# A hybrid attention and RWKV-7 layer on one core: two sets of turned tiles made by VectorE squares and quadrant copies instead of TensorE transposes

## The chip, the cores and the metric

The kernel runs on one core of one Trainium2 chip. The metric is the device time of one execution in microseconds (us). Beside the times there is one profiled execution of the kernel before. Engines are named as in the profile: PE is TensorE (PEld its weight loads), DVE is VectorE, ACT is ScalarE, POOL is GpSimd, SP is the queue that issues nearly all DMAs. L566 is line 566 of the kernel before.

## What is computed

One layer over 256 frames of width 4096, in float32. A single input projection feeds 16 heads of softmax attention with a forget gate, 32 heads of RWKV-7 time mixing (as 16 pairs of 64 wide heads), and a SiLU gate. The gated outputs go through an output projection, then a residual LayerNorm.

```
proj = einsum('bsd,dc->bsc', x, w_in)
logits[t,s] = q_t.k_s/sqrt(128) + sum_{s<j<=t} log f_j      (s <= t)
fox = softmax(logits) @ v
S_t = S_{t-1} diag(decay_t) + (S_{t-1} a_t) b_t^T + v_t k_t^T ;  y_t = S_t r_t
h   = concat(fox, groupnorm(y)*gain + bias + bonus) * silu(z)
x   = LayerNorm(ALPHA*x + h @ w_out)
```

## The kernel before

The input projection is one long stream of matrix products. It is cut into 8 pairs of heads (`n` = 0 to 7) of 4 blocks each (`b` = 0 to 3), and a block into 16 weight tiles (`q`). Block 0 of a pair gives r and k of the RWKV heads, block 1 gives v of both kinds, blocks 2 and 3 give q, k and the gates of the attention heads 2n and 2n+1. Each weight tile is 128x1024 float32. It is loaded by a DMA on SP (`load`, L215), split into a rounded high part by ScalarE (L139, `w_..h`) and a remainder by VectorE (L140, `w_..l`), and used by 12 products of 128x128 on 128x512 (L145 to L147): two of them take the high part for each product that takes the remainder. Four high parts and three remainders can exist at a time, so that the splits run up to three tiles ahead of TensorE. Behind the 8 pairs the output projection follows as a stream of the same kind (`wo`, L872 to L874).

All other work is written as generators, the "sides". `slot()` (L195) lets each of them take one step, and is called after every sixth product of the stream. `yield from wait(n)` therefore lets n slots, or 6n products, pass before the next operation of that side is issued. The table `W` (L46) holds such waits. Each engine then runs its own instructions in one fixed order; a scheduler at build time sets that order, keeping to the program's order for the most part but drawing some instructions forward.

Two sides matter here.

- `rwkv(n)` (L517) handles the RWKV heads of a pair. The chunk factors are in `BK` (128 partitions, 2 halves `u`, 4 chunks `c`, 128 columns). Products `gp` (L531) use them as they are; then POOL scales the first three chunks in place (L533, `kept`). After `W["tp"]` = 4 slots TensorE transposes all eight 128x128 pieces into PSUM (`tp`, L566) and ScalarE copies them out as `BKt` (L567). Then follow the wait `W["d1"]`, 31 steps of a triangular inversion on VectorE (`prod`, `xc`, L595 and L598), one per slot, further products, and for each of the chunks 0 to 2 a product `sp` (L680) that reads `BKt`.
- `fox(i, ...)` (L727) is one attention head. Products `fsp` (L736, L737) give the logits in three 128x128 blocks; VectorE and ScalarE turn them into probabilities in `lg` (L742 to L746). After `W["fp"]` = 5 slots from there TensorE transposes the three blocks into PSUM (`fpt`, L750), ScalarE copies them out as `pT` (L752), and after `W["fo"]` = 3 slots the products `fop` (L756, L757) apply the probabilities to v.

`ident` is an identity matrix, `flat(t)` joins the last two dimensions of a tile, P is 128, B is 32 and NCH is 4. `pst` takes one of five PSUM buffers. `spread` and `gather_heads` already use VectorE's transpose of 32x32 squares, and `gather_heads` (L457) already copies 32 partitions to another 32 on POOL.

Of the kernel before, what the change touches and what calls it, by code (L numbers as in the profile page):

```python
# [10 lines left out]
F32 = mybir.dt.float32  # L11
# [6 lines left out]
P = 128  # L18
# [5 lines left out]
NCH = S // C  # L24
# [18 lines left out]
LAND = 3  # L43
SENT = 3
BEHIND = 13
W = {"fo": 3, "vs": 2, "np": 4, "gp": 5, "tp": 4, "d1": 8, "d2": 12, "xp": 3, "fs": 4, "fp": 5}  # L46
NB = D // OB

PAR = ["w0", "a0", "k_k", "k_a", "r_k", "gn_gain", "gn_bias", "mu_r", "mu_k", "mu_v"]
# [1 line left out]
B = 32  # L51
# [33 lines left out]
def layer(ctx: ExitStack, tc: tile.TileContext, xt, xtok, w_main, w_lora, w_first, muv, w_o, up, par, mulora, fbias, lng, lnb, cst, out):  # L85
    nc = tc.nc
# [8 lines left out]
    def pst(name):  # L95
        return ps.tile([P, 512], F32, tag="ps", name=name)
# [34 lines left out]
    ident = cs[:, C_ID : C_ID + P]  # L131
# [56 lines left out]
    def wait(n):  # L188
        for _ in range(n):
            yield  # L190
# [67 lines left out]
    rp = mid.enter_context(tc.tile_pool(name="rp", bufs=1))  # L258
# [6 lines left out]
    def t256(tag, name, bufs=1):  # L265
        return rp.tile([P, S], F32, tag=tag, name=name, bufs=bufs)
# [103 lines left out]
    def gate(y, key, k):  # L370
        far = k < FAR
        while len(storing) > 1:
            yield
        h = rp.tile([P, S], F32, tag="h", name=f"h{k}")
        nc.vector.scalar_tensor_tensor(h, y, 0.5, szs[key], ALU.mult, ALU.mult)
        pool, tag, bufs = (rp, "hl", 2) if far else (xpool, f"x{k}", 1)
        hl = pool.tile([P, 2, S], F32R, tag=tag, name=f"hl{k}", bufs=bufs)
        nc.scalar.copy(hl[:, 0, :], h)
        nc.vector.tensor_tensor(hl[:, 1, :], h, hl[:, 0, :].bitcast(F32), ALU.subtract)
        if far:  # L380
            storing.append(k)
            yield from wait(SENT)
            issue(hd[k], flat(hl).bitcast(F32))
            kept_h.add(k)
            storing.remove(k)
        else:
            ht[k] = hl
# [3 lines left out]
    def ch(t):  # L391
        return t.rearrange("p (c t) -> p c t", t=C)

    def flat(t):
        return t.rearrange("p a b -> p (a b)")
# [67 lines left out]
    def left(t, j):  # L463
        return t.rearrange("p u c (x j t) -> p u c j x t", x=2, j=2)[:, :, :, j]

    def prepare(i):
# [30 lines left out]
        for j in range(2):  # L497
            h = HALF[j]
            nc.vector.tensor_tensor(BK[h, :, KB[j][1]], ch(k)[h], ch(eI)[h], ALU.mult)
        yield from wait(W["np"] if n else 2 * W["np"])  # L500
        nc.vector.tensor_tensor(hr[:, 0, :], hr[:, 0, :], hr[:, 1, :], ALU.add)
# [15 lines left out]
    def rwkv(n):  # L517
# [4 lines left out]
        lc, BK, LT, bon = q["lc"], q["BK"], q["lt"], q["bon"]  # L522
        lt = [left(LT, j) for j in range(2)]
        yield from wait(W["gp"])
        gp = [[pst(f"gp{n}_{u}_{j}") for j in range(2)] for u in range(2)]
# [18 lines left out]
        nb = rp.tile([P, 2, B, B], F32, tag="Nb", name=f"Nb{n}")  # L544
# [14 lines left out]
        SV = [SVt[:, :, :, j, :] for j in range(2)]  # L559
        UV = [UVt[:, :, :, j, :] for j in range(2)]  # L560
        yield from wait(W["tp"])
        BKt = rp.tile([P, 2, NCH, P], F32, tag="shl", name=f"BKt{n}")
        for u in range(2):
            tp = pst(f"tp{n}_{u}")
            for c in range(NCH):
                nc.tensor.transpose(tp[:, c * P : (c + 1) * P], BK[:, u, c, :], ident)  # L566
            nc.scalar.copy(flat(BKt[:, u]), tp)  # L567
        yield from wait(W["d1"])

        def turns():  # L570
# [41 lines left out]
        for j in range(2):  # L612
# [8 lines left out]
            nc.gpsimd.memset(SV[j][HALF[j], :, 0, :], 0.0)  # L621
        yield from wait(W["d2"] - 1)
        for a in range(4):
# [4 lines left out]
        for u in range(2):  # L628
            for c in range(NCH):
                for j in range(2):  # L630
                    a, b = slice(C * j, C * j + B), slice(C * j + B, C * j + C)
                    nc.tensor.matmul(qp[b, u * P + c * B : u * P + (c + 1) * B], gb[j][a, u, c, B:C], T[a, u, c, :], start=True, stop=True)
        Q = rp.tile([P, 2, NCH, B], F32, tag="xc", name=f"Q{n}")
        for j in range(2):
            b = slice(C * j + B, C * j + C)
# [13 lines left out]

        yield from wait(W["xp"])  # L650
        xp = pst(f"xp{n}")
        for u in range(2):
            for c in range(NCH):
                for j in range(2):
                    a, b = slice(C * j, C * j + B), slice(C * j + B, C * j + C)
                    nc.tensor.matmul(xp[a, u * P + c * B : u * P + (c + 1) * B], Q[b, u, c, :], X[b, u, c, C * j + B : C * j + C], start=True, stop=True)
        for j in range(2):
            a = slice(C * j, C * j + B)
# [68 lines left out]
    def fox(i, q, k, vt):  # L727
        nb = rp.tile([P, 3, P], F32, tag="nb", name=f"nb{i}")
        row = ncd[i : i + 1, :]
        nc.sync.dma_start(out=flat(nb[:, 0:1, :]), in_=row[:, :P].to_broadcast([P, P]))  # L730
        nc.sync.dma_start(out=flat(nb[:, 1:3, :]), in_=row.to_broadcast([P, S]))
        for m in (0, 2):
            nc.gpsimd.affine_select(out=nb[:, m, :], in_=nb[:, m, :], compare_op=ALU.is_ge, fill=NEG, base=0, pattern=[[-1, P]], channel_multiplier=1)  # L733
        yield from wait(W["fs"])
        sp = pst(f"fsp{i}")
        nc.tensor.matmul(sp[:, :P], q[:, :P], k[:, :P], start=True, stop=True)  # L736
        nc.tensor.matmul(sp[:, P : 3 * P], q[:, P:], k, start=True, stop=True)  # L737
        lg = rp.tile([P, 3, P], F32, tag="lg", name=f"lg{i}")
        spv = sp[:, : 3 * P].rearrange("p (a t) -> p a t", t=P)
        st = rp.tile([P, 6], F32, tag="fst", name=f"fst{i}", bufs=2)  # L740
        for m, blk in enumerate((slice(0, 1), slice(1, 3))):
            nc.vector.scalar_tensor_tensor(lg[:, blk, :], spv[:, blk, :], ct[:, m * NF + i : m * NF + i + 1], nb[:, blk, :], ALU.add, ALU.add)  # L742
            nc.vector.tensor_reduce(st[:, m : m + 1], lg[:, blk, :], AX.XY, ALU.max, negate=True)
            nc.scalar.activation(lg[:, blk, :], lg[:, blk, :], AF.Exp, bias=st[:, m : m + 1], accum_out=st[:, 2 + m : 3 + m])
            nc.vector.reciprocal(st[:, 4 + m : 5 + m], st[:, 2 + m : 3 + m])
            nc.vector.tensor_scalar(lg[:, blk, :], lg[:, blk, :], st[:, 4 + m : 5 + m], None, ALU.mult)  # L746
        yield from wait(W["fp"])
        pt = pst(f"fpt{i}")
        for m in range(3):
            nc.tensor.transpose(pt[:, m * P : (m + 1) * P], lg[:, m, :], ident)  # L750
        pT = rp.tile([P, 3 * P], F32, tag="nb", name=f"pT{i}")
        nc.scalar.copy(pT, pt[:, : 3 * P])  # L752
        yield from wait(W["fo"])
        op = pst(f"fop{i}")
        f = slice(i % 2 * P, i % 2 * P + P)
        nc.tensor.matmul(op[:, :S], vt[:, 0, f], pT[:, :S], start=True, stop=False)  # L756
        nc.tensor.matmul(op[:, P:S], vt[:, 1, f], pT[:, S:], start=False, stop=True)  # L757
        o = t256("fq", f"fo{i}")
        nc.scalar.copy(o, op[:, :S])
        while f"f{i}" not in szs or 2 * i >= FAR and not closed:  # L760
            yield
        yield from gate(o, f"f{i}", 2 * i)
        foxed.add(i)
# [6 lines left out]
    def chain():  # L770
        while not ff:
            yield
        yield from forget()
        for n in range(G // 2):
            yield from rwkv(n)
# [12 lines left out]
    def unload(n, b, bk, vt):  # L788
# [43 lines left out]
        else:  # L832
# [4 lines left out]
            yield from wait(LAND - 1)  # L837
        nc.scalar.mul(fq, fq, FOX_SCALE)
        side(fox(i, fq, fk, vt))
        yield  # L840
        silu2(zf, f"f{i}")
# [91 lines left out]
    for b, q in outs:  # L933
        if q == 0:
            pool, tag = (ps, "ps") if b == 1 or b and b % 2 == 0 else (pp, "pp")
# [47 lines left out]
    def moments(m):  # L983
        mv = rpool.tile([P, 2], F32, name=f"mv{m}")
        sd = rpool.tile([P, 1], F32, name=f"sd{m}")
        rs = rpool.tile([P, 1], F32, name=f"rs{m}")
        s2 = rpool.tile([P, 1], F32, name=f"s2{m}")
        zh = rpool.tile([P, 1], F32R, name=f"zh{m}")
        z = factors(m, "d")
        nc.gpsimd.memset(z[:, 3:5], 1.0)  # L990
        za = factors(m, "a") if m else None
        add(m, NB - 1)
        nc.vector.bn_aggr(mv, st[m].rearrange("p b s -> p (b s)"))
        mean = mv[:, 0:1]
        nc.scalar.activation(sd, mv[:, 1:2], AF.Sqrt, bias=lneps)
        nc.vector.reciprocal(rs, sd)
        nc.vector.tensor_tensor(s2, mean, rs, ALU.mult)
        nc.vector.tensor_copy(zh, s2)
        nc.vector.tensor_copy(z[:, 0:3:2], zh.bitcast(F32).to_broadcast([P, 2]))
        last = nc.vector.tensor_tensor(z[:, 1:2], s2, zh.bitcast(F32), ALU.subtract)  # L1000
        if m:
            for n, (v, at) in enumerate(((mean, (slice(0, 3, 2), slice(1, 2))), (sd, (slice(3, 5), slice(5, 6))))):
                h = rpool.tile([P, 1], F32R, name=f"zah{n}")
                nc.scalar.copy(h, v)
                nc.scalar.copy(za[:, at[0]], h.bitcast(F32).to_broadcast([P, 2]))
                nc.scalar.activation(za[:, at[1]], h.bitcast(F32), AF.Identity, scale=-1.0, bias=v)
        rss.append(rs)
        return z, za, last.ins
# [18 lines left out]
    z0, _, last = moments(0)  # L1027
# [23 lines left out]
    for n in range(HALVED):  # L1051
        b = HALVED + n
# [57 lines left out]
```

## Time and profile before

| | us |
|---|---|
| three timed runs | 1934.82, 1935.48, 1938.32; median 1935.48 |
| the profiled execution's own time | 1936.05 |
| its span in the trace | 1934.3 |
| granted TensorE clock, mean | 0.999 of full speed |

The profiled execution took 1.75 us more than its span, which is work outside the recorded stretch. The busy shares of the page say which engine has the most to do, and the list of waits says whether that engine ever stood still; the timeline gives starts in us from the beginning of the span, then durations in us. In the timeline neighbouring equal instructions are merged into one line with their count. A matrix product is listed with a duration that is longer than the distance to the next one, since products overlap.

### The profile page before, as it was taken

The numbers are of one execution on the slowest core, as the hardware profiler recorded it, in microseconds if no ns is written. First come the engines' busy times: TensorE is split into PE (matmuls) and PEld (weight loads), VectorE is DVE, ScalarE is ACT, GpSimd is POOL, SyncE is SP. The second block draws the span as 40 slices with busy tenths as digits, with TensorE's granted clock in tenths as the row PEclk, the third lists the DMA queues.
The fourth block names the chain that finished last, engine by engine and source line by source line (L and its number), as shares of the span: only waits on it lengthen the run. The fifth ranks groups of instructions, "written<-read, shape, count | busy, mean of one in ns | idle before, by whom it ended". The sixth has DMA issues, their size and how long they took to land.

```text
span 1934.3 us, 27820 instructions
## 1 busy us (share of the span) xinstructions
PE 1920.1 (99%) x9897; PEld 1592.7 (82%) x9897; DVE 1362.9 (70%) x2323; ACT 964.2 (50%) x1447; POOL 123.6 (6%) x207
## 2 busy tenths in 40 slices
PE   9999999999999999999999999999999999999998
PEld 9887788888888888888888888888888888888886
DVE  6676777867785778577957795779577856755555
ACT  6554464456444644564446444645454554443332
POOL 0020002000200020002000200020001001000000
PEclk9999999999999999999999999999999999999999
DMA  9577766867786778677867676777677777766564
GB/s 343 151 237 209 220 203 203 241 196 215 214 234 196 216 208 240 190 220 207 235 191 224 208 230 198 223 218 214 207 214 220 241 273 251 245 200 197 186 204 166
DMA packets 269391, 420.04 MB, mean 217 GB/s; under 512 B 142338, under 2 KB 169364, under 8 KB 269252
## 3 DMA queue, kind: packets, MB, share of 16 engines
q1 hardware_dynamic: 268820, 417.58, 70.6%
q8 instruction: 77, 1.26, 0.3%
q10 hardware_dynamic: 432, 0.69, 0.1%
q14 instruction: 62, 0.51, 0.1%
HBM read 388.55 MB, written 29.64 MB: 216 GB/s over the span
## 4 chain that ended last, share of the span: by engine, by line
PE 95%; DVE 2%; DMA 2%; ACT 0%; issue 0%; SPq 0%; DVEq 0%; ACTq 0%
PE acc L145 23%; PE acc L147 23%; PE acc L146 23%; PE oacc L872 6%; PE oacc L874 6%; PE oacc L873 6%; PE up L671 1%; PE gp L531 1%; PE rh L641 1%; PE sp L680 1%; DMA Nb<-nd 0%; PE accl L147 0%; PE accl L146 0%; PE accl L145 0%; PE yp L702 0%; PE yp L700 0%
## 5 line engine op out<-in xcount | busy, mean ns | idle before, releaser
L598 DVE TENSOR_REDUCE xc<-prod 128x8 f32<-128x16 f32 (+30 forms) x248 | 73.1, 295 | 6.5
L595 DVE TENSOR_TENSOR prod<-Nb,xc 128x8 f32<-128x8 f32 (+30 forms) x248 | 71.4, 288 | 6.5 <-DMA Nb<-nd 0.2
L140 DVE TENSOR_TENSOR w_6l<-w,w_6h 128x1024 fp32r<-128x1024 f32 x31 | 37.9, 1221 | 43.1 <-ACT w_6h L139 29.2
L140 DVE TENSOR_TENSOR w_5l<-w,w_5h 128x1024 fp32r<-128x1024 f32 x31 | 41.3, 1333 | 28.2 <-PE acc L147 25.8
L733 POOL TENSOR_SCALAR_AFFINE_SELECT nb<-nb 128x128 f32<-128x128 f32 x32 | 13.8, 436 | 710.3 <-DMA nb<-ncd 265.7
L140 DVE TENSOR_TENSOR w_12l<-w,w_12h 128x1024 fp32r<-128x1024 f32 x31 | 37.9, 1223 | 27.7 <-issue 14.4
L140 DVE TENSOR_TENSOR w_10l<-w,w_10h 128x1024 fp32r<-128x1024 f32 x31 | 37.9, 1222 | 24.3 <-issue 19.7
L139 ACT CAST w_5h<-w 128x1024 fp32r<-128x1024 f32 x31 | 32.6, 1052 | 42.8 <-PE acc L146 37.6
L140 DVE TENSOR_TENSOR w_8l<-w,w_8h 128x1024 fp32r<-128x1024 f32 x31 | 37.8, 1219 | 20.2 <-PE acc L147 10.5
L139 ACT CAST w_13h<-w 128x1024 fp32r<-128x1024 f32 x31 | 32.5, 1047 | 38.0 <-PE acc L146 16.9
L140 DVE TENSOR_TENSOR w_0l<-w,w_0h 128x1024 fp32r<-128x1024 f32 x31 | 37.9, 1223 | 19.1 <-PE acc L147 17.8
L140 DVE TENSOR_TENSOR w_7l<-w,w_7h 128x1024 fp32r<-128x1024 f32 x31 | 37.9, 1221 | 19.0 <-PE acc L147 13.1
L139 ACT CAST w_12h<-w 128x1024 fp32r<-128x1024 f32 x31 | 32.5, 1048 | 37.4 <-DMA w<-in_w_main_dram 21.9
L140 DVE TENSOR_TENSOR w_4l<-w,w_4h 128x1024 fp32r<-128x1024 f32 x31 | 37.8, 1219 | 18.8 <-issue 11.8
L140 DVE TENSOR_TENSOR w_11l<-w,w_11h 128x1024 fp32r<-128x1024 f32 x31 | 37.8, 1220 | 18.1 <-PE acc L147 18.1
L140 DVE TENSOR_TENSOR w_1l<-w,w_1h 128x1024 fp32r<-128x1024 f32 x31 | 37.9, 1223 | 17.9 <-PE acc L147 17.6
L145 PE MATMUL acc<-w_8h,x 128*128 128x512 f32 x124 | 50.4, 407 | 0.0
L145 PE MATMUL acc<-w_7h,x 128*128 128x512 f32 x124 | 49.8, 402 | 0.2 <-ACT w_7h L139 0.2
L145 PE MATMUL acc<-w_5h,x 128*128 128x512 f32 x124 | 49.8, 402 | 0.0
L145 PE MATMUL acc<-w_15h,x 128*128 128x512 f32 x124 | 49.6, 400 | 0.0
L147 PE MATMUL acc<-w_1l,x 128*128 128x512 f32 x124 | 48.5, 391 | 1.1 <-DVE w_1l L140 1.1
L145 PE MATMUL acc<-w_3h,x 128*128 128x512 f32 x124 | 49.5, 399 | 0.0
(814 smaller groups left out, 6543.3 us busy)
## 6 DMA issues: line engine op xcount, KB each, us to landing
w<-in_w_main_dram SPq DMA_DIRECT2D x496, 512.0 KB
wo<-in_w_o_dram SPq DMA_DIRECT2D x128, 512.0 KB
bt<-bk SPq DMA_DIRECT2D x88, 128.0 KB
Nb<-nd SPq DMA_DIRECT2D x16, 512.0 KB
hd<-hl SPq DMA_DIRECT2D x29, 256.0 KB
h<-hd SPq DMA_DIRECT2D x29, 256.0 KB
wr<-in_w_first_dram SPq DMA_DIRECT2D x15, 384.0 KB
lr<-in_w_lora_dram SPq DMA_DIRECT2D x14, 336.0 KB
```

What stands on the lines that cost most here:

```text
L139: nc.scalar.copy(hi[:, :n], src[:, :n])
L140: nc.vector.tensor_tensor(lo[:, :n], src[:, :n], hi[:, :n].bitcast(F32), ALU.subtract)
L145: nc.tensor.matmul(acc[:, :n], xs[k][:, 0, tt], hi[:, o : o + n], start=(k == 0), stop=False)
L146: nc.tensor.matmul(acc[:, :n], xs[k][:, 1, tt], hi[:, o : o + n], start=False, stop=False)
L147: nc.tensor.matmul(acc[:, :n], xs[k][:, 0, tt], lo[:, o : o + n], start=False, stop=(k == KT - 1))
L531: nc.tensor.matmul(o, BK[h, u, c, :], lt[j][h, u, c], start=True, stop=True)
L595: first = nc.vector.tensor_tensor(prod[:, :, :, s + 1 :], nb[:, :, s : s + 1, s + 1 :].to_broadcast([P, 2, NJ, w]), xc[:, :, :, s + 1 :], ...
L598: nc.vector.tensor_reduce(xc[:, :, :, s : s + 1], prod[:, :, :, s:], AX.X, ALU.add)
L641: nc.tensor.matmul(rh[:, u * P : (u + 1) * P], LT[:, u, c, 0:P], flat(SVt[:, u, c]), start=True, stop=True)
L872: nc.tensor.matmul(acc, ht[k][:, 0, tt], hi, start=(k == 0), stop=False)
L873: nc.tensor.matmul(acc, ht[k][:, 1, tt], hi, start=False, stop=False)
L874: nc.tensor.matmul(acc, ht[k][:, 0, tt], lo, start=False, stop=(k == KT - 1))
```

## The change

The two sets of TensorE transposes go. In `rwkv`, VectorE transposes the 32x32 squares of the first three chunks of `BK` in place, once for each `u`. Then 16 POOL copies, one for each pair of a source and a target group of 32 partitions, move the squares to their places in `BKt`, which holds three chunks instead of four. The side yields after 8 of them and again after 16. In `fox`, VectorE transposes the squares of all three blocks of `lg` in place, and 16 copies, taken in turn by ScalarE and POOL, make `pT`. The wait `W["fo"]` ahead of the `fop` products grows from 3 to 7 slots. No PSUM buffer is taken for either set any more.

```diff
-W = {"fo": 3, "vs": 2, "np": 4, "gp": 5, "tp": 4, "d1": 8, "d2": 12, "xp": 3, "fs": 4, "fp": 5}
+W = {"fo": 7, "vs": 2, "np": 4, "gp": 5, "tp": 4, "d1": 8, "d2": 12, "xp": 3, "fs": 4, "fp": 5}
...
-        BKt = rp.tile([P, 2, NCH, P], F32, tag="shl", name=f"BKt{n}")
+        BKt = rp.tile([P, 2, NCH - 1, P], F32, tag="shl", name=f"BKt{n}")
         for u in range(2):
-            tp = pst(f"tp{n}_{u}")
-            for c in range(NCH):
-                nc.tensor.transpose(tp[:, c * P : (c + 1) * P], BK[:, u, c, :], ident)
-            nc.scalar.copy(flat(BKt[:, u]), tp)
+            v = flat(BK[:, u, : NCH - 1, :])
+            nc.vector.transpose(v, v)
+        for a in range(4):
+            for b in range(4):
+                nc.gpsimd.tensor_copy(BKt[B * b : B * (b + 1), :, :, B * a : B * (a + 1)], BK[B * a : B * (a + 1), :, : NCH - 1, B * b : B * (b + 1)])
+            if a % 2:
+                yield
         yield from wait(W["d1"])
...
-        pt = pst(f"fpt{i}")
-        for m in range(3):
-            nc.tensor.transpose(pt[:, m * P : (m + 1) * P], lg[:, m, :], ident)
-        pT = rp.tile([P, 3 * P], F32, tag="nb", name=f"pT{i}")
-        nc.scalar.copy(pT, pt[:, : 3 * P])
+        nc.vector.transpose(flat(lg), flat(lg))
+        pT = rp.tile([P, 3, P], F32, tag="nb", name=f"pT{i}")
+        for a in range(4):
+            for b in range(4):
+                (nc.gpsimd.tensor_copy if b % 2 else nc.scalar.copy)(pT[B * b : B * (b + 1), :, B * a : B * (a + 1)], lg[B * a : B * (a + 1), :, B * b : B * (b + 1)])
+        pT = flat(pT)
         yield from wait(W["fo"])
```

## The prediction

> **What bounds the kernel now.** I read the page first, for the busiest engine and the chain of work that ended last.
>
> ```profile
> span 1934.3 us, 27820 instructions
> PE 1920.1 (99%) x9897; PEld 1592.7 (82%) x9897; DVE 1362.9 (70%) x2323; ACT 964.2 (50%) x1447; POOL 123.6 (6%) x207
> PE 95%; DVE 2%; DMA 2%; ACT 0%; issue 0%; SPq 0%; DVEq 0%; ACTq 0%
> ```
>
> PE is the bound: 95% of the chain is PE. A busy PE can still hide stalls, so the list of PE's waits came next; its longest entries include:
>
> ```profile
> PE acc L147 <- DVE w_1l L140: 1.1, 1, 1.1
> PE acc L147 <- DVE w_8l L140: 1.0, 1, 1.0
> PE xp L656 <- DVE Q L636: 1.0, 1, 1.0
> ```
>
> Each happened once. So PE is fed nearly always, and what leaves PE's queue shortens the kernel, unless the new work elsewhere makes PE wait.
>
> **What is removed from PE.** A product's listed duration isn't its cost, so I took the distance between stream products around each group of transposes from the timeline of PE.
>
> ```profile
> 148.90 0.39 PE L146 MATMUL acc<-w_10h,x 128*128 128x512 f32 x1
> 149.13 0.39 PE L147 MATMUL acc<-w_10l,x 128*128 128x512 f32 x1
> 149.36 1.03 PE L566 MATMUL tp<-cs,BK 128*128 128x128 f32 x8
> 150.15 0.48 PE L145 MATMUL acc<-w_11h,x 128*128 128x512 f32 x1
> 150.47 0.40 PE L146 MATMUL acc<-w_11h,x 128*128 128x512 f32 x1
> ...
> 196.08 0.39 PE L147 MATMUL acc<-w_10l,x 128*128 128x512 f32 x1
> 196.31 0.49 PE L750 MATMUL fpt<-cs,lg 128*128 128x128 f32 x3
> 196.56 0.48 PE L145 MATMUL acc<-w_11h,x 128*128 128x512 f32 x1
> 196.87 0.39 PE L146 MATMUL acc<-w_11h,x 128*128 128x512 f32 x1
> ```
>
> Undisturbed stream products start 0.23 us apart. From 149.13 to 150.47 two distances (0.455) and eight transposes pass, 1.34 us: the eight cost 0.89. From 196.08 to 196.87 it is 0.79: three cost 0.34.
>
> ```profile
> L566 PE MATMUL tp<-cs,BK x64: 270/272/273, 149.4 to 1486.6; 128*128 128x128 f32 x64
> L750 PE MATMUL fpt<-cs,lg x48: 270/272/273, 196.3 to 1586.0; 128*128 128x128 f32 x48
> ```
>
> 64 transposes are 8 groups, 48 are 16 groups: 8 x 0.89 + 16 x 0.34 = 12.5 us off PE. The TensorE page of the Trainium skill ("TensorE: Matmul & The Clock Gate", Part 4: PE-mode transpose) gives about 275 ns for a transpose inside a kernel, for bf16; 112 of them would be 30.8 us, and the result 18 us below mine. The listed 272 ns agrees with it, the distances do not.
>
> **What is added elsewhere.** No DMA is added or moved; SP's queue keeps its order. The new operations' forms aren't in the trace, so their nearest rows bound them.
>
> ```profile
> L492 ACT COPY lc<-eL 128x4 f32<-128x4 f32 x16 | 3.0, 189 | 0.0
> L591 ACT COPY prod<-cs 128x128 f32<-128x128 f32 x16 | 4.0, 296 | 43.7 <-POOL vs L536 43.7
> L620 ACT COPY UV<-SV 64x512 f32<-64x512 f32 x16 | 9.9, 621 | 2.1 <-DVE SV L617 1.6
> L801 DVE STREAM_TRANSPOSE bk<-bk 128x512 f32<-128x512 f32 x44 | 30.8, 702 | 6.6 <-ACT bk L912 4.2 <-ACT bk L910 2.2
> L461 DVE STREAM_TRANSPOSE n<-hr 128x256 f32<-128x256 f32 x16 | 7.1, 442 | 0.3
> L457 POOL COPY hr<-hr x64: 192/376/1384, 99.0 to 1462.8; 32x16 f32<-32x16 f32 x64
> L437 POOL MEMSET eL<- 128x4 f32 x16 | 1.7, 109 | 296.6 <-DVE lt L493 280.8 <-DVE lt L494 15.8
> L263 POOL MEMSET gb<- 128x1024 f32 x2 | 1.9, 964 | 0.0
> ```
>
> An ACT copy of 96 elements lies between 4 and 128 elements: 0.27 us (bounds 0.19 and 0.62). A DVE turn of 384 lies midway between 256 and 512: 0.57. A POOL copy starts from 0.19 for 16 elements, and the two memsets give 0.84 ns for each further element: 0.26 for 96, 0.34 for 192. That is 16 x 0.34 = 5.4 us of POOL per pair for `BKt`, and 8 x 0.26 = 2.1 for each `pT`. The spread of L457 (192 to 1384) has a cause that the timeline shows:
>
> ```profile
> 308.73 1.21 DVE L140 TENSOR_TENSOR w_0l<-w,w_0h 128x1024 fp32r<-128x1024 f32 x1
> 308.94 3.08 POOL L457 COPY hr<-hr 32x16 f32<-32x16 f32 x4 [0.50 <-DVE hr L454]
> 310.74 1.23 DVE L140 TENSOR_TENSOR w_1l<-w,w_1h 128x1024 fp32r<-128x1024 f32 x1
> ```
>
> Four small copies take 3.08 us because two of them overlap a weight split on DVE and end only with it. This is the mechanism of the slower rival below.
>
> For `BKt` the cover is wide. DVE's turn waits for POOL's L533; behind it in DVE's queue stand the next splits, and PE waits for those.
>
> ```profile
> 519.74 1.47 POOL L533 TENSOR_TENSOR BK<-BK,lc 128x768 f32<-128x768 f32 x1 [2.97 <-PE gp L531]
> 526.11 1.21 DVE L140 TENSOR_TENSOR w_9l<-w,w_9h 128x1024 fp32r<-128x1024 f32 x1
> ```
>
> L533 ends at 521.2, and DVE comes to the two turns, which stand before `w_9l`, near 526.1: no wait. The 1.1 us by which `w_9l` moves lies inside the lead of three tiles. The copies end 5 to 22 us (16 x 1.38) later; the first `sp` comes some 54 slots (waits of 8, 12 and 3, and 31 inversion steps) of 6 x 0.2275 us later, 74 us. Cost on PE: 0. With no cover it would be up to 22 us a pair.
>
> For `pT` I followed head 4 (pair 2); the next pairs repeat it.
>
> ```profile
> 573.91 0.38 PE L736 MATMUL fsp<-fk,fq 128*128 128x128 f32 x2
> 580.72 0.34 DVE L746 TENSOR_SCALAR lg<-lg,fst 128x256 f32<-128x256 f32 x1
> 581.40 1.05 ACT L139 CAST w_14h<-w 128x1024 fp32r<-128x1024 f32 x1 [1.47 <-PE acc L146]
> 585.83 0.59 PE L756 MATMUL fop<-pT,vt 128*128 128x256 f32 x2
> ```
>
> The turn ends at 580.72 + 0.34 + 0.57 = 581.6. ACT's eight copies end at 583.8, POOL's at 583.7. `fop` now stands 12 slots behind `fsp`: 573.9 + 0.66 for `fsp` itself + 72 x 0.2275 = 590.9. Slack 7 us. Behind ACT's copies stands `w_14h`; it ends at 584.9 instead of 582.5, its remainder at 586.1, and PE reaches tile 14 one and a half tiles (18 products, 4.1 us) after 585.8, near 589.6. Hidden; the cover goes if an ACT copy takes over 0.7 us. The longer `W["fo"]` delays only the head's output, which is stored for the output projection. The two slots added to `rwkv` move its products as a whole.
>
> **Where PE does wait: the first head.** In the changed program's order of instructions the scheduler has drawn the first `fop` (n = 0) forward: it stands 16 stream products behind `fsp`, not 72. ACT's queue there has seven `pT` copies ahead of `w_9h`, which PE needs for its products 13 to 16.
>
> ```profile
> 186.50 0.74 DVE L742 SCALAR_TENSOR_TENSOR lg<-fsp,ct,nb 128x128 f32<-128x128 f32 x2 [5.88 <-PE fsp L737]
> 187.16 1.22 DVE L140 TENSOR_TENSOR w_8l<-w,w_8h 128x1024 fp32r<-128x1024 f32 x1
> 195.52 0.34 DVE L746 TENSOR_SCALAR lg<-lg,fst 128x256 f32<-128x256 f32 x1
> ...
> 186.99 0.40 PE L146 MATMUL acc<-w_8h,x 128*128 128x512 f32 x1
> 188.43 0.74 PE L147 MATMUL acc<-w_8l,x 128*128 128x512 f32 x2 [1.04 <-DVE w_8l L140]
> 191.64 0.73 PE L147 MATMUL acc<-w_9l,x 128*128 128x512 f32 x2 [0.16 <-DVE w_9l L140]
> ```
>
> In the new order DVE goes from `lg` (186.5) through two reductions (0.5 from start to start), `w_8l` (1.15) and ten short operations (1.9 in all) to the turn: 0.7 + 0.5 + 1.15 + 1.9 = 4.2, so 190.7. Check: before, 9.0 us lie between `lg` and its last scaling; without three splits, one 0.6 us product and five inversion operations that no longer stand between, 3.8 remain. The turn ends at 191.3, seven copies at 193.2, `w_9h` at 194.2. PE, out of work at 187.2, waits 1.7 us for `w_8l` (188.9), runs eight products to 190.7, waits 3.5 for `w_9h`, and finds `pT` done when it comes to `fop` at 195.1. That is 5.2 us of waiting against 1.04 + 0.16 before: +4.0 (with bounds of 0.19 and 0.62 a copy: +3.4 and +6.4; +2.9 if the turn comes 0.5 earlier).
>
> **The last pair.** There ACT's order puts five and three copies of head 15 among the readouts R and UV of the last `rwkv`, whose products follow each other a slot apart. Three copies (0.8) or a cast (1.05) can hold up one such product: +1.0 (bounds 0 and 3; the existing `xp` wait of 1.0 shows the kind).
>
> **Sum.** Against the profiled execution's own 1936.05 us: -12.5 + 4.0 + 1.0 = -7.5, so 1928.5. The median of the runs is 0.57 below that execution: 1928.0. Its own range: 12.5 - 2.9 + 1.1 (if the `w_1l` wait, too, goes with the new order) gives 1924.8; 12.5 - 6.4 - 3 gives 1932.4.
>
> **Rivals.**
>
> *POOL is locked out (slower).* If nearly each `pT` copy meets a two-input operation on DVE, as two of four `hr` copies did, eight cost up to 8 x (1.384 + 0.07) = 11.6 us instead of 2.1, and end at 593.2; `fop` stands at 590.9, so PE waits 2.3. Over the seven even heads after the first that is 16 us: 1928.0 + 16 = 1944. It decides once a copy averages over 1.16 us (9.3 us of slack for eight). For it: DVE is 70% busy, and its splits are two-input. Against it: by the `hr` rate (3.08 for four) eight take 6.2 to 6.8, 2.5 us short of the slack. The Trainium skill's "SBUF — State Buffer" (SBUF: two separate sides) says that whichever of the two starts first holds the shared ports for its whole instruction; the `hr` copies that end with the split agree.
>
> *The gain is eaten (no change).* ACT copies at 0.62, the first head's +6.4, the last pair's +3: 1932.4, and DVE held up by POOL's copies for another 1 us or so: 1933. For it: most 32-partition moves have no row of their own. Against it: ACT's time follows the elements in its rows, and 0.62 belongs to 512.
>
> *Each transpose held PE for its listed 272 ns (much faster).* 112 x 0.272 = 30.5: 1928.0 - 18 = 1910. The distances above speak against it.
>
> **Chances.** Forecast 0.68, locked out 0.14, eaten 0.16, the last 0.02. About 0.2% (3.9 us) can be told from no change, so faster means under 1931.6: 0.70; the same 0.16; slower 0.14. The range runs from 1921.5, some 3 us under the forecast's own for unknown waits that vanish, to 1938, which takes in the eaten case and the first part of the locked-out one; about 0.16 is left out.
>
> **What would show it.** PE should have no `tp` and `fpt`, and some 7500 ns less span; a wait of PE for `w_9h` of 3 to 4 us near 190, and none for `pT` in pairs 1 to 6. `pT` and `BKt` copies on POOL should have minima near 0.26 and 0.34 us and a tail over 1 us. I am wrong if `fop` waits for POOL in each pair, if an ACT copy takes over 0.5 us, or if splits come late in pairs 1 to 6.

## The result, and the profile after

The changed kernel is slower: 1945.7 us (median of six executions, 1943.2 to 1953.6) against 1936.0 for the kernel before on the same chip, a ratio of 1.0049 with a 95% interval of 1.0037 to 1.0062. The prediction was 1928.0, faster, in a range that ended at 1938. The profiled execution has a span of 1942.3 us, 8.0 more than before.

The top of the page of the changed kernel, and the start of its list of PE's waits (us in total, how many, the longest):

```profile
span 1942.3 us, 28013 instructions
PE 1912.6 (98%) x9785; PEld 1583.5 (82%) x9785; DVE 1386.1 (71%) x2355; ACT 983.3 (51%) x1543; POOL 257.5 (13%) x463
```

```profile
PE acc L147 <- DVE w_7l L140: 8.7, 6, 2.0
PE acc L145 <- ACT w_9h L139: 3.4, 1, 3.4
PE oacc L876 <- ACT bk L916: 1.8, 1, 1.8
PE acc L147 <- DVE w_8l L140: 1.6, 1, 1.6
...
PE acc L145 <- ACT w_8h L139: 0.9, 1, 0.9
PE oacc L878 <- DVE wo_3l L140: 0.9, 1, 0.9
```

PE has 112 instructions less and 7.5 us less work, as it should. But it now waits, and the largest entry has a count of six: once in each of pairs 1 to 6, PE waits for the low half of weight tile 7, `w_7l`. No entry names `pT` or `BKt`, and the only one that names POOL is a wait of 1.3 us of the warm-up at the very start, which the kernel before has too.

What stands ahead of `w_7l` is seen on VectorE's timeline (start, duration, engine, line, operation, then the idle time before it and what ended it). First pair 2 of the kernel before: the split with which the inversion's stretch begins, the first inversion step, and `w_7l`; then PE's first use of it.

```profile
534.72 1.23 DVE L140 TENSOR_TENSOR w_12l<-w,w_12h 128x1024 fp32r<-128x1024 f32 x1 [1.50 <-PE acc L147]
535.87 0.17 DVE L595 TENSOR_TENSOR prod<-Nb,xc 128x8 f32<-128x8 f32 x1
...
568.27 1.21 DVE L140 TENSOR_TENSOR w_7l<-w,w_7h 128x1024 fp32r<-128x1024 f32 x1
```

```profile
569.83 0.39 PE L145 MATMUL acc<-w_7h,x 128*128 128x512 f32 x1
...
570.28 0.39 PE L147 MATMUL acc<-w_7l,x 128*128 128x512 f32 x1
```

The same places in the changed kernel:

```profile
544.54 1.23 DVE L140 TENSOR_TENSOR w_13l<-w,w_13h 128x1024 fp32r<-128x1024 f32 x1 [2.14 <-ACT w_13h L139]
545.68 0.32 DVE L598 TENSOR_TENSOR prod<-Nb,xc 128x8 f32<-128x8 f32 x1
...
570.22 1.22 DVE L140 TENSOR_TENSOR w_6l<-w,w_6h 128x1024 fp32r<-128x1024 f32 x1
...
577.23 1.22 DVE L140 TENSOR_TENSOR w_7l<-w,w_7h 128x1024 fp32r<-128x1024 f32 x1
```

```profile
576.12 0.39 PE L145 MATMUL acc<-w_7h,x 128*128 128x512 f32 x1
...
578.50 0.50 PE L147 MATMUL acc<-w_7l,x 128*128 128x512 f32 x1 [1.77 <-DVE w_7l L140]
```

The reader is to see two lengths. From the first of those splits to `w_7l`, VectorE works through inversion steps and splits without a pause: 33.6 us before, 32.7 after (no row between them names idle time). From the same split to PE's first product of tile 7 there were 35.1 us before (569.83 - 534.72) and there are 31.6 after (576.12 - 544.54). The stretch hardly changed; the time it has did. Before, `w_7l` was ready at 569.5, 0.8 us ahead of its product; worked out in the same way, the margin over pairs 1 to 6 was 0.4 us on average, and in pair 4 below nothing (there, and in pair 5, the stretch also has 0.4 and 0.2 us of idle time). The changed kernel begins the inversion behind `w_13l` instead of `w_12l`, one tile (2.73 us, 12 products of 0.2275) later against PE's products, and saves one split (1.14) in return. In pair 2 another 0.8 us was lost ahead of the stretch, where `w_13l` waited 2.14 us for its high part; over the six pairs this varies, and on average it is 0.4.

The program's order of instructions says the same without times. On VectorE, with the splits as numbers (13 is `w_13l`) and each inversion step as R, other work left out, pairs 1 to 6:

```
before  12 RRRR 13 RRR 14 RRR 15 RRR 0 RRR 1 RR 2 RR 3 RR 4 RR 5 RR 6 RRRRR   7 8
after   13 RRRR 14 RRR 15 RRR 0 RRR 1 RR 2 RR 3 RRR 4 RR 5 RR 6 RRRRRRR 7 8
```

In both orders the end of the inversion is drawn ahead of `w_7l`; what is left of it at that point grew from five steps to seven. So there were two theories. **A, the order:** the two empty slots (`yield`) among the `BKt` copies push the inversion 12 products back against the stream, and the scheduler's order then makes `w_7l` late in each pair and draws the first `fop` forward; the turns and copies themselves cost nothing. **B, the copies:** POOL's copies hold VectorE up, or ACT's hold the casts up, and the slots are harmless.

### The profile page after: what moved, and what is told of

The parts are those of the page before. It is cut to its first block, busy times and chain, and to the rows that moved or that the text cites. A ratio compares the mean times of both kernels' runs of the same rounds, so it can differ in the third digit from the quotient of the medians.

```text
span 1942.3 us, 28013 instructions
## 1 busy us (share of the span) xinstructions
PE 1912.6 (98%) x9785; PEld 1583.5 (82%) x9785; DVE 1386.1 (71%) x2355; ACT 983.3 (51%) x1543; POOL 257.5 (13%) x463
## 5 line engine op out<-in xcount | busy, mean ns | idle before, releaser
L755 POOL COPY pT<-lg 32x96 f32<-32x96 f32 x128 | 50.0, 391 | 454.5 <-DVE lg L751 449.8
L568 POOL COPY BKt<-BK 32x192 f32<-32x192 f32 x128 | 77.4, 605 | 54.2 <-DVE BK L565 49.2
L140 DVE TENSOR_TENSOR w_13l<-w,w_13h 128x1024 fp32r<-128x1024 f32 x31 | 38.6, 1244 | 26.1 <-ACT w_13h L139 11.5
L147 PE MATMUL acc<-w_7l,x 128*128 128x512 f32 x124 | 48.3, 400 | 8.8 <-DVE w_7l L140 8.7
L140 DVE TENSOR_TENSOR w_12l<-w,w_12h 128x1024 fp32r<-128x1024 f32 x31 | 38.8, 1253 | 21.7 <-PE acc L147 11.5
L139 ACT CAST w_1h<-w 128x1024 fp32r<-128x1024 f32 x31 | 32.7, 1055 | 40.5 <-PE acc L146 19.2
L145 PE MATMUL acc<-w_9h,x 128*128 128x512 f32 x124 | 49.8, 402 | 3.4 <-ACT w_9h L139 3.4
L736 POOL TENSOR_SCALAR_AFFINE_SELECT nb<-nb 128x128 f32<-128x128 f32 x32 | 18.5, 578 | 236.7 <-DMA nb<-ncd 214.1
L147 PE MATMUL acc<-w_8l,x 128*128 128x512 f32 x124 | 48.3, 393 | 1.6 <-DVE w_8l L140 1.6
```

The costliest lines, as they stand in the source:

```text
L139: nc.scalar.copy(hi[:, :n], src[:, :n])
L140: nc.vector.tensor_tensor(lo[:, :n], src[:, :n], hi[:, :n].bitcast(F32), ALU.subtract)
L145: nc.tensor.matmul(acc[:, :n], xs[k][:, 0, tt], hi[:, o : o + n], start=(k == 0), stop=False)
L147: nc.tensor.matmul(acc[:, :n], xs[k][:, 0, tt], lo[:, o : o + n], start=False, stop=(k == KT - 1))
L568: nc.gpsimd.tensor_copy(BKt[B * b : B * (b + 1), :, :, B * a : B * (a + 1)], BK[B * a : B * (a + 1), :, : NCH - 1, B * b : B * (b + 1)])
L755: (nc.gpsimd.tensor_copy if b % 2 else nc.scalar.copy)(pT[B * b : B * (b + 1), :, B * a : B * (a + 1)], lg[B * a : B * (a + 1), :, B * b : ...
```

## The experiments

Each time is a median, beside the kernel before on the same chip; a ratio is to that kernel, with its 95% interval.

**The two slots alone, in the kernel before** (`e1_two_waits`).

```diff
             nc.scalar.copy(flat(BKt[:, u]), tp)
+        yield
+        yield
         yield from wait(W["d1"])
```

> The kernel before, with two empty slots added behind the TensorE transposes of BK: no transpose leaves PE, and nothing is copied on POOL. Theory A (the order: the two added slots move the inversion by 12 products against the weight splits, the scheduler then puts seven inversion steps in a row ahead of w_7l on DVE where five stood, and draws the first fop forward): PE waits about 1.8 us for w_7l in each of six pairs (11 us) and about 5 us more in the first head, so 1936 + 11 + 5 = 1952, at least 1945. Theory B (the copies: POOL's copies hold DVE's splits up, or ACT's copies hold ACT's casts up): there are none here, so 1936 within 2, and no wait for w_7l over 0.5 us.

1950.9 us against 1937.7, ratio 1.0060 (1.0048 to 1.0073). Not an operation was added or removed, and the kernel lost more than the whole change loses. Its list of PE's waits begins:

```profile
PE acc L147 <- DVE w_7l L140: 6.7, 6, 1.7
PE oacc L874 <- ACT bk L914: 2.1, 1, 2.1
PE acc L147 <- DVE w_8l L140: 1.6, 1, 1.6
```

Theory A holds against B: 1952 had been stated for it, 1936 for B. Its terms fit less well than its sum. The six waits are 6.7 us by this list and 7.6 by the distances between PE's starts, where 11 were stated, and the first head lost 1.2 us instead of 5 (from its first `fsp` to tile 3 of the next block 36.06 us against 34.91). The wait for `bk` near the end, which the changed kernel has too, was not stated at all; here it comes with the slots alone. The profiled execution is one of the faster ones (1947.1), and what the other 4 us of the median are isn't shown.

**The whole change with the slots taken back** (`e2_d1_six`).

```diff
-W = {"fo": 7, "vs": 2, "np": 4, "gp": 5, "tp": 4, "d1": 8, "d2": 12, "xp": 3, "fs": 4, "fp": 5}
+W = {"fo": 7, "vs": 2, "np": 4, "gp": 5, "tp": 4, "d1": 6, "d2": 12, "xp": 3, "fs": 4, "fp": 5}
```

> The changed kernel whole, with the wait d1 cut from 8 slots to 6, so that the inversion stands where it stood before the change; every copy and turn stays. Theory A (the order): the six waits for w_7l (11.1 us by start distances) and the first head's loss (about 5 us) go, and 1945.7 becomes 1945.7 - 11 - 5 = 1929.5, within 3. Theory B (the copies): all copies are still there, so PE still waits for w_7l in each pair and the time stays at 1943 to 1947.

1926.2 us, ratio 0.9943 (0.9931 to 0.9956). Every turn and copy is still there; five steps stand ahead of `w_7l` again, and the first `fop` is back in its place, 78 products behind the last `fsp` in the trace (16 in the changed kernel, 72 in the later heads of both). This is 3.3 us below what theory A stated. The wait for `bk` near the end went as well (0.2 instead of 1.8), which is about half of that. The kernel is faster than both others. Its largest waits in the stream of weight tiles, near the size of those in the kernel before:

```profile
PE acc L147 <- DVE w_1l L140: 1.5, 1, 1.5
...
PE acc L147 <- DVE w_8l L140: 1.0, 1, 1.0
PE acc L147 <- DVE w_7l L140: 0.9, 2, 0.6
```

**Each half alone.** The `BKt` half keeps the old probabilities (`fpt`, `fo` = 3); the probabilities' half keeps the old `tp` and adds no slots.

```diff
-W = {"fo": 7, ...
+W = {"fo": 3, ...
...
-        nc.vector.transpose(flat(lg), flat(lg))
...
+        pt = pst(f"fpt{i}")
...
```

> The BK part alone: turn on DVE, 16 POOL copies, the two slots; the probabilities by TensorE as before. Theory A (the order): the order of DVE's splits against the inversion is that of the changed kernel, so w_7l is late by about 1.8 us in six pairs and the first head loses some 4 us; 1936 - 7.1 (64 transposes) + 11 + 4 = 1944, within 3. Theory B with POOL's BK copies as the cause: the same 1944 with the waits right behind the copies and not 40 us later at w_7l. Theory B with the pT copies as the cause: 1936 - 7.1 = 1929.

> The probabilities' part alone: turn on DVE, eight copies each on ACT and POOL, fo = 7; BK by TensorE as before, no added slots. Theory A (the order): 1936 - 5.4 (48 transposes) = 1930.5, within 2, no repeated wait of PE. Theory B with the pT copies as the cause: slower than 1936, with a wait of PE for w_7l or for a cast in each pair.

The `BKt` half, which holds the slots: 1944.8, ratio 1.0040 (1.0026 to 1.0054), with six waits for `w_7l` of 11.1 us in all. The probabilities' half: 1931.8, ratio 0.9972 (0.9962 to 0.9983), with `w_7l` at 0.3 us. Its gain of 5.9 us is that of the 48 transposes (5.4 in the prediction). Both times came out as theory A says, but not every term did: in the `BKt` half the first head lost 1.2 us, as in `e1_two_waits`, where 4 were stated. In both of these kernels the first `fop` is drawn forward too (12 products behind `fsp`), but the seven `pT` copies that stand on ACT ahead of `w_9h` are missing, and with them the long wait for `w_9h`. So the first head's loss needs the slots and the copies together, while the waits for `w_7l` need the slots alone.

**More slots, and fewer** (`e5_d1_ten`, `e8_d1_four`): the same line as in `e2_d1_six`, with 10 and with 4 for `d1`. In the program's order nine (in pair 1 eleven) and three steps then stand ahead of `w_7l`.

> The changed kernel with d1 = 10 instead of 8: the inversion moves by another 12 products, and nine inversion steps stand between w_6l and w_7l on DVE (five before the change, seven with it). Theory A (the order): each step is a product and a reduction, 0.8 us at this width, so w_7l comes another 1.6 us later in each of six pairs: waits of about 3.4 us each instead of 1.8, 1945.7 + 10 = 1955, within 4. If the number of steps ahead of w_7l did not set the wait (rival: any of the two shifts disturbs once, or the copies do it), 1945.7 within 2.

> The changed kernel with d1 = 4: three inversion steps stand between w_6l and w_7l. Theory A: the two small waits for w_7l that are left with d1 = 6 (0.9 us in all) go too, so 1925.3, within 1.5; the first head's fop stays in its place. Against it: the first fsp now stands 6 products later and the loads' order on SP shifts, so that other splits may come late: 1927 to 1932.

With 10: 1957.2, ratio 1.0099 (1.0086 to 1.0112). With 4: 1928.1, ratio 0.9951 (0.9939 to 0.9963), no better than 6 although no wait for `w_7l` is left. The first entry of the first list, and entries of the second:

```profile
PE acc L147 <- DVE w_7l L140: 19.6, 6, 6.8
```

```profile
PE zp L1016 <- DVE zd L1004: 1.4, 1, 1.4
...
PE xp L659 <- DVE Q L639: 1.1, 1, 1.1
```

Three, five, seven and nine steps give waits for `w_7l` of 0, 0.9, 8.7 and 19.6 us. The wait follows the number of steps in the way, with two reservations: 6.8 of the 19.6 us belong to pair 1 with its eleven steps (the other five pairs have 2.6 each, against 1.4 with seven), and with `d1` = 4 the order on PE changed too, so that four products of `w_7h` instead of two stand ahead of the first of `w_7l`. For `d1` = 4 the stated gain of 1 us did not show; its runs scatter by more than that (1924.9 to 1932.0), and what else it costs stays open.

**The first head by itself.** One pair gets the slots, the others don't, and the reverse.

```diff
-        yield from wait(W["d1"])
+        yield from wait(6 if n else W["d1"])      # e9_only_head
+        yield from wait(W["d1"] if n else 6)      # e6_first_head, e10_first_head_again
```

> The changed kernel with d1 = 8 for the first pair only and 6 for the others: the first fop is drawn forward as in the changed kernel, and five inversion steps stand ahead of w_7l in pairs 1 to 6 as before the change. Theory A with the two losses independent: 1926.2 + 4.4 (the first head's gaps by start distances, 8.9 against 4.5) = 1930.6, within 1.5. Rival: a stall of PE early is made up later, because the loads run ahead in it: 1926 to 1928.

> The changed kernel with d1 = 6 for the first pair of heads only and 8 for the others: the first fop stands where it belongs again, 72 products behind its fsp, while seven inversion steps still stand ahead of w_7l in pairs 1 to 6. Theory A: the waits for w_8l and w_9h near 190 fall back to 1.0 and 0.2, some 5 us go, the six waits for w_7l (11.1 us by start distances) stay: 1945.7 - 5 = 1941, within 1.5. If the first head's loss were made up later anyway: 1945; if it were the larger part: under 1937.

> The kernel of e6_first_head once more (d1 = 6 for the first pair, 8 for the others), for its waits in a second profile. If the loss of 4.4 us that it mends was given back because its six waits for w_7l are longer in every execution (rival: the loads are later against PE when PE doesn't stall first): 1945 to 1947 again, and waits for w_7l over 12 us again. If the long waits of that one profile (13.3 us, in the longest of its runs) were its own: waits for w_7l of 8 to 11 us, and a median of 1941 to 1944.

`e9_only_head`: 1931.5, ratio 0.9974 (0.9965 to 0.9983), 5.3 us above `e2_d1_six`. With the copies in place the first head's loss is real, and nothing makes it up later. Its largest waits are those that the changed kernel has there:

```profile
PE acc L145 <- ACT w_9h L139: 3.4, 1, 3.4
PE acc L147 <- DVE w_8l L140: 1.6, 1, 1.6
```

`e6_first_head` missed: 1946.7, ratio 1.0049 (1.0037 to 1.0061), where 1941 was expected. The same kernel again gave 1942.9, ratio 1.0034 (1.0022 to 1.0047), as stated for the case that the long waits of the first profile, the slowest of its six executions, were its own. The row for `w_7l` in the first and in the second profile:

```profile
PE acc L147 <- DVE w_7l L140: 13.3, 6, 4.0
```

```profile
PE acc L147 <- DVE w_7l L140: 10.2, 6, 2.3
```

The waits for `w_7l` aren't a fixed price. In pair 1 the stretch began at 348.4 in the first profile, after ACT had waited 4.42 us for the load of tile 13; in the second it began at 345.6. What the load of one tile takes moves the whole stretch. And a long wait costs more than itself (last section), which makes up most of the difference between the two profiles. Against the changed kernel's ratio of 1.0049 the first head's repair thus gained nothing in the first set of runs and 2.9 us in the second, with intervals of some 0.0012 to either side of each ratio. What it is worth while the six waits are there stays open; without them it is the 5.3 us of `e9_only_head`.

**The POOL copies of `BKt` twice** (`e7_copies_twice`), on top of `d1` = 6.

```diff
                 nc.gpsimd.tensor_copy(BKt[B * b : B * (b + 1), :, :, B * a : B * (a + 1)], BK[B * a : B * (a + 1), :, : NCH - 1, B * b : B * (b + 1)])
+                nc.gpsimd.tensor_copy(BKt[B * b : B * (b + 1), :, :, B * a : B * (a + 1)], BK[B * a : B * (a + 1), :, : NCH - 1, B * b : B * (b + 1)])
```

> The changed kernel with d1 = 6, and each of the 16 POOL copies of BKt issued twice with the same result: 128 POOL copies more. If POOL's copies are hidden and disturb DVE only inside the lead of the splits (the prediction's cost of nothing): as with d1 = 6 alone, 1926.2 within 1.5. If they hold DVE up (the rival of the locked-out POOL, from the other side): 128 copies of 0.34 us are 43 us of shared time, of which 1 us a pair or more should reach PE as waits for w_9l to w_12l: 1934 or more.

1932.0, ratio 0.9969 (0.9958 to 0.9981): 5.8 us slower than `e2_d1_six`. Neither of the two outcomes stated came: the copies do reach PE, but at `w_7l`, 22 us behind the last of them, and not at `w_9l` to `w_12l`. The waits for `w_7l` are 5.2 us in all, against 0.9, and the wait for `bk` near the end is back with 1.7 us, so that it doesn't need the moved inversion. VectorE's rows of pair 2, with the copies once and twice:

```profile
532.50 1.39 DVE L140 TENSOR_TENSOR w_12l<-w,w_12h 128x1024 fp32r<-128x1024 f32 x1 [1.42 <-PE acc L147]
...
537.92 0.16 DVE L598 TENSOR_TENSOR prod<-Nb,xc 128x48 f32<-128x48 f32 x1
...
566.54 1.22 DVE L140 TENSOR_TENSOR w_7l<-w,w_7h 128x1024 fp32r<-128x1024 f32 x1
```

```profile
534.68 1.35 DVE L140 TENSOR_TENSOR w_12l<-w,w_12h 128x1024 fp32r<-128x1024 f32 x1 [2.31 <-ACT w_12h L139]
...
540.04 0.33 DVE L599 TENSOR_TENSOR prod<-Nb,xc 128x48 f32<-128x48 f32 x1
...
569.44 1.21 DVE L140 TENSOR_TENSOR w_7l<-w,w_7h 128x1024 fp32r<-128x1024 f32 x1
```

POOL had begun two copies at 539.59; the product that meets them takes 0.33 instead of 0.16 us. Nothing in this pair's stretch is idle, so what lengthens its first third delays its end. From `w_12l` to `w_7l` it lasts, averaged over pairs 1 to 6, 33.8 us before the change, 34.2 with the copies once and 35.0 with the copies twice; `w_7l` is then 0.4 early, just in time, and 1.0 late. So the copies as the change has them eat most of the margin at `w_7l`, and doubled they overdraw it. Theory A's second half, that the copies cost nothing, is true only as long as there is a margin.

**All probabilities' copies on one engine** (`e11_pt_all_act`, `e12_pt_all_pool`), on top of `d1` = 6.

```diff
-                (nc.gpsimd.tensor_copy if b % 2 else nc.scalar.copy)(pT[...], lg[...])
+                nc.scalar.copy(pT[...], lg[...])            # e11_pt_all_act
+                nc.gpsimd.tensor_copy(pT[...], lg[...])     # e12_pt_all_pool
```

> The changed kernel with d1 = 6 and all 16 pT copies on ACT, none on POOL: 16 x 0.27 = 4.3 us stand ahead of one cast of a weight tile instead of 2.2. By the prediction's break point (eight copies of 0.7 us, 5.6 us, before the cover of a cast goes) this is still hidden: 1926.2 within 1.5, no wait of PE for a cast in the even heads. If the cover is thinner than that: a wait for w_14h or w_15h of 1 us or so in each of 15 heads, 1931 or more.

> The changed kernel with d1 = 6 and all 16 pT copies on POOL: 16 x 0.39 (their mean in the changed kernel, tail included) = 6.3 us from the turn to the last copy, against a slack of 7.0 + 2.3 = 9.3 us to fop. Hidden: 1926.2 within 1.5, no wait for pT. If POOL is locked out as in the prediction's slower rival (a copy of 16 averages over 0.58 us): a wait of PE for pT in each pair, 1930 or more.

All on ACT: 1928.5, ratio 0.9963 (0.9950 to 0.9975), 2.3 us above `e2_d1_six` and a little outside what was stated; no wait returns in each head, there are two single ones behind ACT's `bk` copies (1.3 and 1.0 us). All on POOL: 1938.3, ratio 1.0007 (0.9999 to 1.0016). The wait in that kernel, and head 4 in it; then head 4 with the copies shared (`e2_d1_six`):

```profile
PE fop L760 <- POOL pT L755: 9.3, 7, 1.4
...
584.76 8.58 POOL L755 COPY pT<-lg 32x96 f32<-32x96 f32 x16 [44.19 <-DVE lg L751]
...
593.39 0.70 PE L760 MATMUL fop<-pT,vt 128*128 128x256 f32 x2 [1.36 <-POOL pT L755]
```

```profile
581.57 5.28 POOL L755 COPY pT<-lg 32x96 f32<-32x96 f32 x8 [44.15 <-DVE lg L751]
...
588.68 0.59 PE L760 MATMUL fop<-pT,vt 128*128 128x256 f32 x2
```

Sixteen copies take 8.58 us, 0.54 each, and hold PE up in seven heads. Eight take 5.28, 0.66 each, and end 1.8 us ahead of `fop`. The slack from turn to `fop` was also smaller here than the 9.3 us of the prediction: the turn ended at 584.7 and `fop` could have started at 592.0 (593.39 - 1.36), 7.3 us. The prediction's slower rival exists, and the change with its copies shared stays just on the safe side of it.

## Why the prediction was wrong, step by step

*What bounds the kernel* was right, and so were the **transposes removed**. The half with the probabilities gained 5.9 us for a predicted 5.4; with the inversion's place as before, the whole change gained 11.5 (1937.7 to 1926.2) for 12.5 less what the longer stretch gives back. 30.5 us, by the listed 272 ns, is out.

*The prices* were right as medians. In the changed kernel's answers for the tiles, each with the shortest, the median and the longest of one (ns):

```profile
L755 ACT COPY pT<-lg x128: 253/270/273, 191.8 to 1592.2; 32x96 f32<-32x96 f32 x128
L755 POOL COPY pT<-lg x128: 258/262/1163, 191.8 to 1590.7; 32x96 f32<-32x96 f32 x128
L568 POOL COPY BKt<-BK x128: 337/342/2314, 152.2 to 1503.5; 32x192 f32<-32x192 f32 x128
L751 DVE STREAM_TRANSPOSE lg<-lg x16: 567/574/579, 191.2 to 1586.1; 128x384 f32<-128x384 f32 x16
```

0.27, 0.26, 0.34 and 0.57 us had been worked out from neighbouring rows, and the tails over 1 us were foreseen. The tails weigh: on average a POOL copy took 0.39 us for `pT` and 0.61 for `BKt`.

*The first head* was right in kind: a wait for `w_9h` of 3.37 us (3.5 predicted) and for `w_8l` of 1.56 (1.7). Its price was 4.0, and measured it is 4.7 (from the first `fsp` to the first product of tile 3 in the next block 39.29 us against 34.91, and 0.34 for the three transposes that are gone), or 5.3 by `e9_only_head`; the bounds reached to 6.4. PE's rows there show what was left out: right after the long wait the products follow each other at 0.43 us instead of 0.23, and from 194.9 to 198.3 the granted clock is 0.50 (last section).

```profile
194.84 0.80 PE L145 MATMUL acc<-w_9h,x 128*128 128x512 f32 x1 [3.37 <-ACT w_9h L139]
195.43 0.63 PE L146 MATMUL acc<-w_9h,x 128*128 128x512 f32 x1
195.86 0.63 PE L145 MATMUL acc<-w_9h,x 128*128 128x512 f32 x1
```

*`pT` in the steady pairs* was right for the changed kernel: no wait. (The 589.6 at which PE was to reach tile 14 is 589.9 by the prediction's own terms, and in the kernel before it was 590.6, so the cover there was larger than stated.)

*The last pair* was given 1.0 us for a readout held up by `pT` copies, and that wait came, with 0.8 us for `R` and 0.2 for `UV`:

```profile
1586.75 1.40 ACT L755 COPY pT<-lg 32x96 f32<-32x96 f32 x5 [0.34 <-issue]
...
1591.40 0.26 ACT L647 COPY R<-rh 64x128 f32<-64x128 f32 x1
```

```profile
1591.71 0.66 PE L674 MATMUL up<-R,X 128*128 128x64 f32 x4 [0.77 <-ACT R L647]
```

ACT is busy from the five copies (1.40 us) to `R`, and `e1_two_waits`, which has the slots but no `pT` copies on ACT, has no such wait. What was not foreseen stands ahead of it, at 1565: the wait of 1.8 us for ACT's `bk` copies.

**The step that failed** is one sentence: "The two slots added to `rwkv` move its products as a whole." They do, but the inversion isn't only PE's products; it is 31 steps on VectorE, in one queue with the splits that feed PE, and the place of those steps against the splits moved with the slots. So the sum has no term for the six waits for `w_7l`: the cost of the `BKt` half on PE was put at 0. The prediction looked at the turns in VectorE's queue (1.1 us, inside the lead of three tiles at `w_9l`, which is true at that place) and at the order on PE and ACT, and didn't set the splits against the inversion's end, 40 us later. The trace of before had what was needed: the stretch without idle time, and `w_7l` ready only 0.8 us ahead of its product. The prediction named "splits come late in pairs 1 to 6" as what would refute it, and that is what happened.

In the profiled execution the forecast missed by 15.5 us (8.0 more instead of 7.5 less). By the distances between PE's starts, the six waits for `w_7l` are 9.7 of it (2.35, 2.16, 1.53, 1.78, 1.84 and 1.42, less 0.23 each); a stretch at half the clock behind the first of them about 1.6; the first head 0.7 more than priced; the last pair 0.9 more than its term (the wait for `bk` 1.9, while the `xp` wait of 1.0 that the kernel before has went); single waits for `w_8h` near 94 and `wo_3l` near 1673 another 2.1. That is 15.0, nearly all of it. Why those last two came wasn't tried.

The rival of the locked-out POOL gave 1944, close to what was measured, by a mechanism that isn't the cause: no `fop` waits in the changed kernel. A time that fits does not make a cause.

## What to carry to other kernels

An empty slot is an edit like any other: where a scheduler orders the work, two of them can cost more than 112 transposes gain, so the order on every engine is set against the old one around whatever the edit moves, to the end of the chain it moves and not only beside it. Where an engine works through a long stretch without idle time, its last product's margin is the margin of the whole stretch; look there first for what a later start or a little more work will break. And when a change misses, undo its waits and its work separately: here one constant changed from 8 to 6 turned a loss of 0.5% into a gain of 0.6%.

## What the runs showed of the hardware

**A wait of PE of about 2 us can be paid for twice.** After the first wait for `w_7l` in the changed kernel the products first follow each other at 0.23 us, and then at 0.43, when the granted clock falls to half (second view: a window and its length, then busy time and count for PE, PEld, DVE, ACT and POOL, then the granted clock):

```profile
384.55 0.50 PE L147 MATMUL acc<-w_7l,x 128*128 128x512 f32 x1 [1.96 <-DVE w_7l L140]
...
385.81 0.46 PE L146 MATMUL acc<-w_7h,x 128*128 128x512 f32 x1
386.06 0.63 PE L147 MATMUL acc<-w_7l,x 128*128 128x512 f32 x1
386.49 0.63 PE L145 MATMUL acc<-w_7h,x 128*128 128x512 f32 x1
```

```profile
384.60:386.00 1.40, 1.40 (x6) 1.18 (x7) 1.36 (x2) 0.00 (x1) 0.00 (x0) 1.00 0.38 73
386.00:389.40 3.40, 3.40 (x9) 2.67 (x9) 1.65 (x2) 3.24 (x4) 0.00 (x0) 0.50 0.79 271
```

In the traces' clock records each such stretch inside the kernel lasts 3.41 us, or twice that. In the profile of `e6_first_head` PE ran for 18.6 us in five of them, in that of its repetition for 6.8 us in two; at 0.43 instead of 0.23 us a product that is about 8.7 and 3.2 us lost (estimates). These 5.5 us, and 3.1 from the waits for `w_7l` themselves (13.3 against 10.2), account for the 8.6 between the two spans (1949.7 and 1941.1). Over all fourteen profiles, no wait in the stream of weight tiles that left under 2.2 us between two starts was followed by such a stretch; of those between 2.2 and 3.2 us 12 of 17 were, and all five longer ones.

Which waits are punished can be read from the records too. Within a profile the stretches begin a whole number of steps of 3.413 us apart (in the changed kernel at 194.86 and 386.00, 56 steps). Cut into such windows, the fourteen profiles (without the first 10 and the last 15 us) have 16 windows in which PE, by the listed durations, had no product for 1.9 us or more in all, and half the clock followed each of them; it followed 3 of 7 windows with 1.7 to 1.9 us, and 3 of some 7800 with less. So it matters less how long a wait is than how much of it falls into one window.

The Trainium skill describes a clock gate that looks at free-running windows of about 3.4 us and halves PE's clock after an idle one ("TensorE: Matmul & The Clock Gate", Part 1: The HAM clock gate). The 3.41 us, the granted 0.50 and 0.43 against 0.23 agree with it; that a little over half a window without products was enough is what the rows add.

**A POOL copy and a VectorE product with two inputs hold each other up in both directions.** In the rows of `e7_copies_twice` the product took 0.33 instead of 0.16 us when a copy was under way, and in the changed kernel copies of 0.26 and 0.34 us took up to 1.16 and 2.31 beside VectorE's work. The Trainium skill has the rule ("SBUF — State Buffer", SBUF: two separate sides): the two share a pair of ports, and whichever starts first holds it for its whole instruction. The rows agree.
